# A two-layer hybrid trunk on one core: layer 0's activation rows split by ScalarE and an adding transfer, and its wide products in runs of three

## The chip, the cores and the metric

The kernel runs on one core of a Trainium2 chip. The metric is the device time of one execution in microseconds; the time of a version is the median over its runs. One further execution is recorded by the hardware profiler, and every statement on where time goes is read from that record. The engines are named as the profile names them: PE is TensorE (matrix products; PEld is its loading of weights), DVE is VectorE, ACT is ScalarE, POOL is GpSimd, SP is SyncE, which here only issues transfers.

## The reference

A decoder trunk of two layers over 512 positions of width 1024, in float32. Each layer is a mixer and then a gated feed-forward network with a causal convolution of width 3, both behind an RMS norm and added to the residual. The change lies in the feed-forward network of layer 0:

```python
def gated_conv_ffn(x, w_gate, w_up, conv_w, conv_b, w_down):
    g = jnp.einsum('bsd,df->bsf', x, w_gate)
    g = causal_dwconv3(g, conv_w) + conv_b
    up = jnp.einsum('bsd,df->bsf', x, w_up)
    return jnp.einsum('bsf,fd->bsd', jax.nn.silu(g) * up, w_down)
...
def reference(x, ...):
    h = x
    for layer in range(DEPTH):
        ...
        hn = rms_norm(h, norm_ffn[layer])
        h = h + gated_conv_ffn(hn, w_ffn_gate[layer], w_ffn_up[layer], ...)
    return rms_norm(h, final_norm)
```

D_FF is 2816, that is 22 rows of 128 features. In the kernel a row is a tile of 128 features by 512 positions.

## The kernel before

**Numbers in two parts.** A float32 operand is multiplied as a high part (rounded to the format float32r) plus a low part (the rest, rounded likewise): high x high, high x low and low x high are added up in PSUM. Every operand of a product therefore exists as two tiles, `..._hi` and `..._lo` (weights: `whi_...`, `wlo_...`). There are two ways to make them. In the first, ScalarE copies the source into the high tile and VectorE subtracts: low = source - high (functions `split`, L262, `halves`, L855, and `parts`, L148). In the second, ScalarE copies the source times -1 into the low tile, a transfer on POOL's queue adds the source to it, and ScalarE makes the high tile as well (functions `summed`, L137, and the inner `split` of `prepare`, L884). VectorE has no part in the second.

**The feed-forward stage.** `Ffn.steps` (L1004) runs over the 22 rows two at a time: group f makes the rows f and f+1. Group 0 is computed directly; the groups 2 to 20 are done by a seven-product scheme for two-by-two blocks, once for the gate (`g`) and once for the up-projection (`u`), so 14 products a group. `prepare` builds a group's weight operands (`whi_a`, `whi_s12g`, `wlo_u` and so on) and `products` (L912) runs the 14 products in the order of its list `todo`: g1, u1, g2, g5, g6, u5, u6, g7, u2, u7, g3, u3, g4, u4. The results collect in PSUM banks that are named after gate or up-projection, group and bank, such as `g_10a`; products 1, 6, 7 and 4 of the gate follow each other in the same bank, so each must be taken out (ScalarE's COPY at L944 and VectorE's add at L932) before the next one writes. Each matmul of a product covers a quarter of the contraction.

**Narrow and wide.** A narrow product (L705) issues three matmuls of 256 columns for each quarter. A wide product (L695) issues one of 512 columns for each quarter, in which the high weights meet the high and low parts of the moving operand side by side, and one of 256 columns with the low weights. In layer 0 the products are wide from group 8 on, in part in group 6 (`FIRST_WIDE`, L675); in layer 1 from group 6 on. The order of the two widths is set by the list `parts_of`. Layer 0 alternates: wide, narrow, narrow, wide, and so on, product by product. Layer 1 runs three products' low weights, then three products' high weights.

**After the products.** VectorE and ScalarE turn the gate into a row: multiply by the norm's factor (L968), convolution (`c`, L739 and L741), Silu (`s`, L749), and products with the up-projection (L976 to L983). `STEPS` (L667) says when finished rows become operands: `act` (L752) splits a row `s` into `a_hi` and `a_lo`. Rows 0 and 1 are split after group 0, rows 2 and 3 after group 2, rows 4 and 5 after group 4, then four rows at a time: 6 to 9 after group 8, 10 to 13 after group 12, 14 to 17 after group 16, 18 to 21 at the end. The tiles `a_hi` and `a_lo` have four buffers each. The down-projection of a set of rows (`half_down`, matmuls `d<-a_hi,whi_d` and so on, L156 to L158) comes in two halves, one behind each of the next two groups: rows 6 to 9 are read behind group 10 and again behind group 12.

**What sets the order.** The order of the instructions on each engine is made by a scheduler when the program is built, within the limits of the data and of a few explicit orders (`behind`, L81, which says that one instruction stands after another of the same engine). Each engine then runs its list strictly in order, and waits where an operand or a buffer is not ready. POOL's queue issues the adding transfers in order as well.

Of the kernel before, what the change touches and what calls it, by code (L numbers as in the profile page):

```python
# [9 lines left out]
F32R = mybir.dt.float32r  # L10
BF16 = mybir.dt.bfloat16
AF = mybir.ActivationFunctionType
ALU = mybir.AluOpType
PSUM = bass.MemoryType.PSUM

P = 128
D = 1024
S = 512
# [3 lines left out]
NF = FF // P  # L22
# [9 lines left out]
def tile_trunk(ctx: ExitStack, tc: tile.TileContext, x, norm_mix, norm_ffn, final_norm,  # L32
# [3 lines left out]
    nc = tc.nc  # L36
# [44 lines left out]
    def behind(ins, first):  # L81

        if first is not None:
            tc.add_manual_dep(ins.ins, first.ins.name, mybir.DependencyInfo(
                mybir.DependencyClass.NoSync, mybir.DependencyReason.DATA), reason="order")
# [176 lines left out]
    def split(pool, src, name, scale=1.0, tag="a", bufs=None):  # L262
        hi = pool.tile([P, S], F32R, tag=f"{tag}hi", bufs=bufs, name=f"{name}_hi")
        lo = pool.tile([P, S], F32R, tag=f"{tag}lo", bufs=bufs, name=f"{name}_lo")
        nc.scalar.activation(hi, src, AF.Copy, scale=scale)  # L265
        if isinstance(scale, float):
            nc.vector.tensor_tensor(lo, src, hi.bitcast(F32), ALU.subtract)
        else:
            nc.vector.scalar_tensor_tensor(lo, src, scale, hi.bitcast(F32),
                                           op0=ALU.mult, op1=ALU.subtract)  # L270
        return hi, lo
# [15 lines left out]
    def padded_tile():  # L287
        turn[0] += 1
        return padded[turn[0] % NPADDED]
# [426 lines left out]
    class Ffn:  # L716
# [33 lines left out]
            return s  # L750

        def act(self, ft, s):  # L752
            self.acts[ft] = split(self.ap, s, f"a{self.layer}_{ft}", tag="a", bufs=4)

        def pair_weights(self, order):

# [155 lines left out]
        def products(self, f, stat):  # L912

            layer, ap, n = self.layer, self.ap, f"{self.layer}_{f}"
            banks = {"g": {}, "u": {}}
            kept = ap.tile([P, 3, HALF], F32, tag="kept", bufs=1, name=f"kept{n}")
            pads = [padded_tile() for _ in range(2)]
            lo, hi = slice(2, 2 + HALF), slice(2 + HALF, 2 + S)
            dst = {("g", 1): pads[0][:, lo], ("g", 6): pads[0][:, hi], ("g", 7): pads[1][:, hi],
                   ("g", 4): pads[1][:, lo]}  # L920
            dst.update({("u", product): kept[:, i, :] for i, product in enumerate((1, 6, 7))})
            onto = {2: 1, 7: 7, 3: 6}
            s = {}

            def in_both(key, product):
                first = FIRST_WIDE[layer]
                return f >= first[key] or f == first["g"] and product in (2, 5, 3)

            def add(d, bank, halves):
                ins = None  # L930
                for half in halves:
                    ins = nc.vector.tensor_tensor(d, bank[:, half * HALF : (half + 1) * HALF], d,  # L932
                                                  ALU.add)
                return ins

            def after(key, product, bank):
                halves = range(1 + in_both(key, product))
                if product in onto:
                    ins = add(dst[key, onto[product]], bank, halves)
                    if product == 7:  # L940
                        self.added[key] = ins
                elif (key, product) != ("u", 4):
                    d = dst[key, 7 if product == 5 else product]
                    nc.scalar.copy(d, bank[:, :HALF])  # L944
                    add(d, bank, halves[1:])

            todo = [("g", 1), ("u", 1), ("g", 2), ("g", 5), ("g", 6), ("u", 5), ("u", 6),
                    ("g", 7), ("u", 2), ("u", 7), ("g", 3), ("u", 3), ("g", 4), ("u", 4)]
            if layer and all(in_both(*at) for at in todo):
                parts_of = [(0, (False,))]  # L950
                for i in range(0, len(todo), 3):
                    parts_of += [(j, (True,)) for j in range(i, min(i + 3, len(todo)))]
                    parts_of += [(j, (False,)) for j in range(i + 1, min(i + 4, len(todo)))]
            else:
                parts_of = [(i, (i % 2 == 1, i % 2 == 0)) for i in range(len(todo))]
            begun = set()
            for i, lows in parts_of:
                key, product = todo[i]
                bank = self.multiply(banks[key], f"{key}{n}", product, stat[key, product],
                                     in_both(key, product), lows)  # L960
                if len(lows) == 1 and i not in begun:
                    begun.add(i)
                    continue
                after(key, product, bank)
                if (key, product) in (("g", 4), ("g", 3)):
                    j = product == 4
                    row = pads[j][:, 2:]
                    nc.vector.tensor_tensor(row, row, self.r, ALU.mult)  # L968
                    s[j] = self.silu(self.conv(pads[j], f + j), f + j)
                    if j and layer == 0:  # L970
                        nc.vector.tensor_tensor(s[1], s[1], self.r, ALU.mult)
            if layer == 0:
                nc.vector.tensor_tensor(kept[:, :2, :], kept[:, :2, :],
                                        self.r.rearrange("p (a b) -> p a b", a=2), ALU.mult)
            s0 = s[0].rearrange("p (a b) -> p a b", a=2)
            nc.vector.tensor_tensor(s0, kept[:, :2, :], s0, ALU.mult)  # L976
            nc.vector.tensor_tensor(s[1][:, HALF:], kept[:, 2, :], s[1][:, HALF:], ALU.mult)
            last = bank[:, :HALF]
            if in_both("u", 4):
                last = kept[:, 0, :]  # L980
                nc.scalar.copy(last, bank[:, :HALF])
                add(last, bank, (1,))
            nc.vector.tensor_tensor(s[1][:, :HALF], last, s[1][:, :HALF], ALU.mult)  # L983
            return [(f + 1, s[1]), (f, s[0])]
# [358 lines left out]
    def ffn1(norm):  # L1343
        with tc.tile_pool(name="f1", bufs=1) as ap:
# [108 lines left out]
            def product(p, i, c0=0, c1=512, bank=None):  # L1453
# [14 lines left out]
                return ps  # L1468

            vec, act, pool = nc.vector, nc.scalar, nc.gpsimd  # L1470
            rows_f = [wp.tile([P, D], F32, tag="raw", bufs=4, name=f"yf{t}") for t in range(NT)]
            factor, root = ([ssf[:, t, i : i + 1] for t in range(NT)] for i in (4, 5))
# [91 lines left out]
            refined(0, 1)  # L1564
            taken(7, 1, right)
            scaled(act, 0, left)
            scaled(act, 0, right)
            stored(0, slice(0, D))
            all_but_last(2, right)
# [84 lines left out]
```

## Time and profile before

| | us |
|---|---|
| median of 3 runs (lowest, highest) | 966.77 (966.71, 966.88) |
| the profiled execution | 966.66 |
| its span, first to last instruction | 964.9 |
| first product of the feed-forward stage's groups of layer 0, group 2 | 165.8 |
| last down-projection of that stage begins | 461.1 |

The clock granted to TensorE was 0.999 of full speed over the span. The page calls an engine busy while an instruction of its own runs; a busy TensorE is not TensorE at its peak, so besides its busy share the distances between the starts of its matmuls are read. Idle time of another engine costs nothing unless TensorE waits for it.

### The profile page before, as it was taken

To read this page: it belongs to the slowest core of one execution; us is meant where nothing else is said; L and a number is where in the kernel's file an instruction comes from. 1 tells how busy PE (TensorE), PEld (TensorE's weight loads), DVE (VectorE), ACT (ScalarE), POOL (GpSimd) and SP (SyncE) were. 2 spreads that over 40 slices of the span, in tenths; PEclk is the share of its full clock that TensorE was granted. 3 is DMA by queue.
4 is the path that set the end of the run, shared out by engine and by line. 5 is a ranking of instruction groups with operands and counts; after the bars stand their busy time and mean duration, and the time that the engine had idled before them with its cause. 6 is when DMAs were issued, how large, how long until landed. Compare 5 with 4: busy or idle time off the path is not lost.

```text
span 964.9 us, 14240 instructions
## 1 busy us (share of the span) xinstructions
PE 956.6 (99%) x5155; PEld 826.5 (86%) x5155; DVE 847.2 (88%) x1435; ACT 620.8 (64%) x944; POOL 162.4 (17%) x183
## 2 busy tenths in 40 slices
PE   9999999999999999999999999999999999999997
PEld 7888898998888888888888888989888888888885
DVE  6887988989899998998878689889998989989898
ACT  5524667766576565765487847787765566646676
POOL 2142333111011010110311002321111011110124
PEclk9999999999999999999999999999999999999999
DMA  7442345777777578774452323467776777667865
GB/s 253 146 141 87 66 144 120 179 188 178 176 174 176 153 175 197 164 180 137 131 153 88 109 88 88 138 134 184 186 181 175 182 176 174 167 168 177 207 146 152
DMA packets 95538, 150.47 MB, mean 156 GB/s; under 512 B 5252, under 2 KB 61548, under 8 KB 95468
## 3 DMA queue, kind: packets, MB, share of 16 engines
q1 hardware_dynamic: 77996, 98.69, 32.8%
q0 software_dynamic: 15696, 49.03, 27.8%
q10 hardware_dynamic: 1776, 1.84, 0.6%
q8 instruction: 41, 0.67, 0.3%
q14 instruction: 29, 0.24, 0.1%
HBM read 98.42 MB, written 2.10 MB: 104 GB/s over the span
## 4 chain that ended last, share of the span: by engine, by line
PE 99%; DMA 0%; DVE 0%; issue 0%; SPq 0%; ACT 0%; DVEq 0%
PE dn L156 3%; PE d L157 3%; PE d L156 3%; PE dn L157 3%; PE d L158 3%; PE dn L158 3%; PE vu_a L1166 2%; PE gu L156 2%; PE gu L158 2%; PE gu L157 2%; PE u_2a L705 1%; PE g_2a L705 1%; PE u_4a L705 1%; PE g_6a L695 1%; PE u_12a L695 1%; PE u_16a L695 1%
## 5 line engine op out<-in xcount | busy, mean ns | idle before, releaser
L143 POOL DMA_DIRECT2D wlo_g<-raw_g x20 | 17.2, 860 | 318.8 <-ACT wlo_g L141 66.5
L741 DVE SCALAR_TENSOR_TENSOR c<-rows,prm,c 128x512 f32<-128x512 f32 x88 | 64.9, 746 | 1.2 <-ACT c L739 1.0
L156 PE MATMUL d<-a_hi,whi_d 128*128 128x512 f32 x144 | 56.1, 389 | 0.0
L156 PE MATMUL dn<-whi_dn,a_hi 128*128 128x512 f32 x144 | 56.1, 389 | 0.0
L157 PE MATMUL d<-a_lo,whi_d 128*128 128x512 f32 x144 | 56.1, 389 | 0.0
L157 PE MATMUL dn<-wlo_dn,a_hi 128*128 128x512 f32 x144 | 56.0, 389 | 0.0
L158 PE MATMUL d<-a_hi,wlo_d 128*128 128x512 f32 x144 | 56.0, 389 | 0.0
L158 PE MATMUL dn<-whi_dn,a_lo 128*128 128x512 f32 x144 | 56.0, 389 | 0.0
L856 ACT ACTIVATE whi_a<-raw_g 128x512 fp32r<-128x512 f32 x20 | 12.6, 632 | 67.2 <-PE g_18e L695 9.4
L739 ACT ACTIVATE c<-rows,prm 128x512 f32<-128x512 f32 x44 | 31.3, 714 | 10.2 <-DVE rows L968 10.1
L1371 DVE SCALAR_TENSOR_TENSOR y<-dn,small,y 128x512 f32<-128x512 f32 x40 | 28.0, 749 | 6.7 <-PE dn L158 6.7
L749 ACT ACTIVATE s<-c,prm 128x512 f32<-128x512 f32 x44 | 31.4, 715 | 3.2 <-DVE c L741 3.0
L265 ACT ACTIVATE a_hi<-s 128x512 fp32r<-128x512 f32 x40 | 24.7, 626 | 12.2 <-PE d L158 9.4
L201 ACT ACTIVATE hg<-h,prm 128x512 fp32r<-128x512 f32 x24 | 17.2, 719 | 23.5 <-DVE h L314 17.0
L158 PEld LDWEIGHTS dn<-whi_dn,a_lo 128*128 128x128 f32 x144 | 27.0, 188 | 5.7
L158 PEld LDWEIGHTS d<-a_hi,wlo_d 128*128 128x128 f32 x144 | 27.0, 188 | 5.6
L157 PEld LDWEIGHTS dn<-wlo_dn,a_hi 128*128 128x128 f32 x144 | 27.0, 188 | 5.6
L156 PEld LDWEIGHTS d<-a_hi,whi_d 128*128 128x128 f32 x144 | 27.0, 188 | 5.6
L156 PEld LDWEIGHTS dn<-whi_dn,a_hi 128*128 128x128 f32 x144 | 27.0, 188 | 5.6
L157 PEld LDWEIGHTS d<-a_lo,whi_d 128*128 128x128 f32 x144 | 27.0, 188 | 5.5
L141 ACT ACTIVATE wlo_g<-raw_g 128x1024 fp32r<-128x1024 f32 x20 | 21.0, 1048 | 16.3 <-PE g_2e L705 7.6
L152 DVE TENSOR_TENSOR wlo_d<-raw_d,whi_d 128x1024 fp32r<-128x1024 f32 x18 | 22.0, 1224 | 10.4 <-ACT whi_d L151 10.4
(1279 smaller groups left out, 3377.6 us busy)
## 6 DMA issues: line engine op xcount, KB each, us to landing
raw_g<-in_w_ffn_gate_dram SPq DMA_DIRECT2D x40, 512.0 KB, 3.8
raw_u<-in_w_ffn_up_dram SPq DMA_DIRECT2D x40, 512.0 KB, 3.7
raw_dn<-in_w_ffn_down_dram SPq DMA_DIRECT2D x22, 512.0 KB, 3.5
wlo_g<-raw_g POOLq DMA_DIRECT2D x20, 512.0 KB, 5.2
wlo_u<-raw_u POOLq DMA_DIRECT2D x20, 512.0 KB, 6.1
raw_d<-in_w_ffn_down_dram SPq DMA_DIRECT2D x18, 512.0 KB, 4.1
wlo_s12g<-s12g POOLq DMA_DIRECT2D x18, 512.0 KB, 6.6
wlo_s34g<-s34g POOLq DMA_DIRECT2D x18, 512.0 KB, 6.2
```

Source lines behind the costliest of these rows:

```text
L141: first = nc.scalar.activation(lo, raw, AF.Copy, scale=-1.0)
L152: behind(nc.vector.tensor_tensor(lo, raw, hi.bitcast(F32), ALU.subtract), after[0])
L156: nc.tensor.matmul(ps, lhs[0], rhs[0], start=start, stop=False, skip_group_check=skip)
L157: nc.tensor.matmul(ps, lhs[0], rhs[1], start=False, stop=False, skip_group_check=skip)
L158: nc.tensor.matmul(ps, lhs[1], rhs[0], start=False, stop=stop, skip_group_check=skip)
L265: nc.scalar.activation(hi, src, AF.Copy, scale=scale)
L695: last_matmul[0] = nc.tensor.matmul(ps if low else banks[at], left(kp)[low], right(kp)[0] if low else both(kp), start=first, stop=kp == NP ...
L705: nc.tensor.matmul(ps, l, r, start=first, stop=end, skip_group_check=True)
L739: nc.scalar.activation(c, t[:, 0:S], AF.Copy, scale=prm("cf", ft))
L741: self.last_conv = nc.vector.scalar_tensor_tensor(c, t[:, i : S + i], prm("cf", i * NF + ft), c, op0=ALU.mult, op1=ALU.add)
L749: self.last_silu = nc.scalar.activation(s, c, AF.Silu, bias=self.prm("bf", ft))
L1371: return nc.vector.scalar_tensor_tensor(dst, ps, ffn.cols[:, t : t + 1], dst, op0=ALU.mult, op1=ALU.add)
```

## The change

For the rows 0 to 17 of layer 0, `act` makes the parts in the second way: ScalarE copies the row times -1 into `a_lo`, a transfer on POOL's queue adds the row to it, and ScalarE copies the row into `a_hi`, in that order. The tiles and their four buffers stay the same; rows 18 to 21 and layer 1 keep VectorE's subtraction. And `products` uses the order in runs of three products also in layer 0, in every group whose products are all wide but the last: the groups 8, 10, 12, 14, 16 and 18.

```diff
@@ -750,7 +750,16 @@
         def act(self, ft, s):
-            self.acts[ft] = split(self.ap, s, f"a{self.layer}_{ft}", tag="a", bufs=4)
+            name = f"a{self.layer}_{ft}"
+            if not (self.layer == 0 and ft < NF - 4):
+                self.acts[ft] = split(self.ap, s, name, tag="a", bufs=4)
+                return
+            hi = self.ap.tile([P, S], F32R, tag="ahi", bufs=4, name=f"{name}_hi")
+            lo = self.ap.tile([P, S], F32R, tag="alo", bufs=4, name=f"{name}_lo")
+            first = nc.scalar.activation(lo, s, AF.Copy, scale=-1.0)
+            nc.gpsimd.dma_start(lo, s, accum_op=ALU.add)
+            behind(nc.scalar.activation(hi, s, AF.Copy), first)
+            self.acts[ft] = hi, lo
@@ -946,7 +955,7 @@
             todo = [("g", 1), ("u", 1), ("g", 2), ("g", 5), ("g", 6), ("u", 5), ("u", 6),
                     ("g", 7), ("u", 2), ("u", 7), ("g", 3), ("u", 3), ("g", 4), ("u", 4)]
-            if layer and all(in_both(*at) for at in todo):
+            if (layer or f + 2 < NF) and all(in_both(*at) for at in todo):
                 parts_of = [(0, (False,))]
                 for i in range(0, len(todo), 3):
                     parts_of += [(j, (True,)) for j in range(i, min(i + 3, len(todo)))]
```

Lines behind L762 move down by nine, and the scheduler puts other instructions in another order too. Three places follow; rows of the changed kernel carry its own line numbers.

ScalarE before, from the COPY that empties the last bank of group 8 to the COPY of the first bank of group 10 (`g_10a`) and the two copies behind it. `a_6_hi` to `a_9_hi` are the rows' high parts, the other `whi_...` and `wlo_...` are group 10's weights:

```order
L981 COPY kept_8_2603<-u_8a 128x256
L749 ACTIVATE s_9_2752<-c_9_2748,prm_415 128x512
L265 ACTIVATE a_6_hi<-s_6_2436 128x512
L265 ACTIVATE a_9_hi<-s_9_2752 128x512
L887 ACTIVATE wlo_s34g_10_2884<-s34g_10_2868 128x1024
L889 ACTIVATE whi_s34g_10_2883<-s34g_10_2868 128x1024
L141 ACTIVATE wlo_u_10_1_2894<-raw_u_10_1_2859 128x1024
L265 ACTIVATE a_8_hi<-s_8_2725 128x512
L944 COPY rows_119<-g_10a 128x256
L856 ACTIVATE whi_s12u_10_2891<-s12u_10_2888 128x1024
L145 ACTIVATE whi_u_10_1_2893<-raw_u_10_1_2859 128x1024
```

And with the change, from the same COPY to the COPY of `g_10a`:

```order
L990 COPY kept_8_2609<-u_8a 128x256
L759 ACTIVATE a_6_lo<-s_6_2442 128x512
L761 ACTIVATE a_6_hi<-s_6_2442 128x512
L898 ACTIVATE whi_s34g_10_2893<-s34g_10_2878 128x1024
L141 ACTIVATE wlo_u_10_1_2904<-raw_u_10_1_2869 128x1024
L759 ACTIVATE a_9_lo<-s_9_2758 128x512
L761 ACTIVATE a_9_hi<-s_9_2758 128x512
L865 ACTIVATE whi_s12u_10_2901<-s12u_10_2898 128x1024
L759 ACTIVATE a_8_lo<-s_8_2735 128x512
L761 ACTIVATE a_8_hi<-s_8_2735 128x512
L145 ACTIVATE whi_u_10_1_2903<-raw_u_10_1_2869 128x1024
L953 COPY rows_119<-g_10a 128x256
```

The low parts are copied ahead of the high ones, and `whi_s12u` and `whi_u`, which stood behind the COPY of `g_10a`, now stand ahead of it. Ahead of this piece stand, in the new order, `a_7_lo`, the Silu `s_8`, `a_7_hi`, `wlo_s34g` and the Silu `s_9`; `s_8` stood ahead of `a_7_hi` before. The groups 14 and 18 read alike with their own numbers.

TensorE in group 6, around the second use of the bank `g_6a` (product 6 of the gate, `g_6a<-t`), before:

```order
L695 MATMUL g_6e<-t_0_3_1609,whi_s12g_6_2270 128x512
L695 MATMUL u_6e<-t_0_0_1558,wlo_s12u_6_2291 128x256
L695 MATMUL u_6e<-t_0_1_1576,wlo_s12u_6_2291 128x256
L695 MATMUL u_6e<-t_0_2_1594,wlo_s12u_6_2291 128x256
L695 MATMUL u_6e<-t_0_3_1609,wlo_s12u_6_2291 128x256
L695 MATMUL u_6e<-t_0_0_1558,whi_s12u_6_2290 128x512
L695 MATMUL g_6a<-t_0_1556,whi_s12g_6_2270 128x512
```

And with the change:

```order
L695 MATMUL g_6e<-t_0_2_1594,whi_s12g_6_2276 128x512
L695 MATMUL g_6e<-t_0_3_1609,whi_s12g_6_2276 128x512
L695 MATMUL g_6a<-t_0_1556,whi_s12g_6_2276 128x512
L695 MATMUL g_6a<-t_1_1574,whi_s12g_6_2276 128x512
L695 MATMUL g_6a<-t_2_1592,whi_s12g_6_2276 128x512
```

The five matmuls of `u_6e` that stood ahead of `g_6a` now come behind that product. On ScalarE the copies `a_5_lo`, `a_5_hi`, `a_4_lo` and `a_4_hi` stand directly ahead of the COPY that empties `g_6a`, where `a_5_hi` and `a_4_hi` stood; on VectorE the subtractions `a_5_lo` and `a_4_lo`, which stood ahead of its add into `rows` from `g_6a`, are gone.

POOL's transfers from the second weight operand of group 10 on, before:

```order
L888 DMA wlo_s34g_10_2884<-s34g_10_2868 128x1024
L143 DMA wlo_u_10_1_2894<-raw_u_10_1_2859 128x1024
L143 DMA wlo_g_12_1_3161<-raw_g_12_1_3144 128x1024
L888 DMA wlo_s12g_12_3159<-s12g_12_3154 128x1024
L888 DMA wlo_s34g_12_3171<-s34g_12_3155 128x1024
```

And with the change:

```order
L897 DMA wlo_s34g_10_2894<-s34g_10_2878 128x1024
L760 DMA a_6_lo<-s_6_2442 128x512
L143 DMA wlo_u_10_1_2904<-raw_u_10_1_2869 128x1024
L760 DMA a_9_lo<-s_9_2758 128x512
L760 DMA a_8_lo<-s_8_2735 128x512
L143 DMA wlo_g_12_1_3171<-raw_g_12_1_3154 128x1024
```

The transfer of row 7 stands ahead of this piece, the one of row 6 between two weight operands of group 10, and those of rows 9 and 8 behind them.

## The prediction

> **What bounds the kernel now.** I read the page's busy times and its chain of waits first, to see which engine sets the end.
>
> ```profile
> PE 956.6 (99%) x5155; PEld 826.5 (86%) x5155; DVE 847.2 (88%) x1435; ACT 620.8 (64%) x944; POOL 162.4 (17%) x183
> ...
> PE 99%; DMA 0%; DVE 0%; issue 0%; SPq 0%; ACT 0%; DVEq 0%
> ```
>
> TensorE (PE) works 956.6 of 964.9 us and the chain that ended last is 99% TensorE: the other engines matter only where they make it wait. The change lies in layer 0's feed-forward stage, so next come the busy times of that stretch, and of the same stage of layer 1, which already runs its wide groups in runs of three. The columns are the stretch, its length, then busy time and count of PE, PEld, DVE, ACT and POOL, the clock, the DMA share and GB/s.
>
> ```profile
> 160.00:461.00 301.00, 300.96 (x1709) 264.61 (x1708) 276.40 (x488) 195.17 (x282) 31.82 (x37) 1.00 0.70 172
> 640.00:940.00 300.00, 300.00 (x1653) 261.98 (x1652) 272.26 (x485) 197.15 (x291) 36.97 (x43) 1.00 0.73 176
> ```
>
> TensorE is idle for 0.04 of 301 us there, at full granted clock. So this stage gains only by cheaper matmuls or by removing the rare slow spots inside the pipeline. Of waits that end on other engines, two are recorded: one at the start of the program, one in the wide-matmul line (L695).
>
> ```profile
> PE z L417 <- ACT whi_z L410: 0.3, 1, 0.3
> ...
>   DVE rows L932: 0.4, 1
> ```
>
> **Part 1, runs of three products.** No product is added or removed; matmuls of equal width stand together longer, so TensorE changes width less often. Layer 0's group 12 (first six rows, the last being what follows it) and layer 1's group 10 (last three) show both orders with the same 14 wide products; columns are start, duration, operation.
>
> ```profile
> 308.89 1.07 PE L695 MATMUL g_12a<-hg,whi_a 128*128 128x512 f32 x4
> 309.80 0.64 PE L695 MATMUL g_12a<-hg,wlo_a 128*128 128x256 f32 x4
> 310.27 0.64 PE L695 MATMUL u_12a<-hg,wlo_a 128*128 128x256 f32 x4
> 310.75 1.09 PE L695 MATMUL u_12a<-hg,whi_a 128*128 128x512 f32 x4
> 311.68 1.07 PE L695 MATMUL g_12b<-hg,whi_g 128*128 128x512 f32 x4
> ...
> 328.44 0.39 PE L156 MATMUL d<-a_hi,whi_d 128*128 128x512 f32 x1
> ...
> 756.20 1.07 PE L695 MATMUL g_10a<-hg,whi_a 128*128 128x512 f32 x4
> ...
> 760.38 1.07 PE L695 MATMUL g_10e<-t,whi_s12g 128*128 128x512 f32 x4
> ...
> 775.71 0.39 PE L156 MATMUL dn<-whi_dn,a_hi 128*128 128x512 f32 x1
> ```
>
> Layer 0: 328.44 - 308.89 = 19.55 us. Layer 1: 775.71 - 756.20 = 19.51 us. The row at 310.75 shows why: a wide run behind a narrow one takes 0.93 us to the next start (311.68), one at the head 0.91 (308.89 to 309.80), so each change of width costs 0.02 us and layer 1 has two fewer (five for seven). Groups 8, 10, 12, 14, 16 and 18 change: 6 x 0.04 = **-0.24 us** (bounds by the rows' rounding, -0.18 to -0.30).
>
> [...]
>
> **Part 2, the rows' low parts.** Eighteen rows (0 to 17) lose a VectorE subtraction and gain a ScalarE copy and an adding transfer from POOL's queue. Prices:
>
> ```profile
> L267 DVE TENSOR_TENSOR a_lo<-s,a_hi x40: 679/684/693, 177.5 to 879.2; 128x512 fp32r<-128x512 f32 x40
> ...
> L265 ACT ACTIVATE a_hi<-s 128x512 fp32r<-128x512 f32 x40 | 24.7, 626 | 12.2 <-PE d L158 9.4
> ...
> L143 POOL DMA_DIRECT2D wlo_g<-raw_g x20 | 17.2, 860 | 318.8 <-ACT wlo_g L141 66.5
> ...
> t<-t POOLq DMA_DIRECT2D x4, 256.0 KB, 3.7
> ...
> wlo_s12g<-s12g POOLq DMA_DIRECT2D x18, 512.0 KB, 6.6
> ...
> q0 software_dynamic: 15696, 49.03, 27.8%
> ```
>
> VectorE loses 18 x 0.684 = 12.3 us of its 276.4; ScalarE gains 18 x 0.626 = 11.3 (195 to 206 of 301); POOL gains 18 x 0.86 = 15.5 (32 to 47). The transfers move 18 x 0.262 = 4.7 MB; at q0's rate that is 4.7/49.03 x 27.8% x 964.9 = 26 us of all 16 engines, which takes the DMA share from 0.70 to about 0.79. A row of 256 KB has no row of its own on this path: between the 3.7 us of the 256 KB transfers and the 6.6 us of the 512 KB ones I take 5. None of this is on TensorE, so its price is 0 where cover holds. Three places decide.
>
> *Group 6.* Here stands the 0.4 us wait. Bank g_6a must be emptied by VectorE before TensorE's product 6 writes it.
>
> ```profile
> 222.69 0.63 PE L695 MATMUL u_6e<-t,wlo_s12u 128*128 128x256 f32 x4
> 223.16 0.40 PE L695 MATMUL u_6e<-t,whi_s12u 128*128 128x512 f32 x1
> 223.60 1.19 PE L695 MATMUL g_6a<-t,whi_s12g 128*128 128x512 f32 x4
> ...
> 219.69 1.14 ACT L265 ACTIVATE a_hi<-s 128x512 fp32r<-128x512 f32 x2
> 220.73 0.35 ACT L944 COPY rows<-g_6a 128x256 f32<-128x256 f32 x1
> ...
> 220.72 1.29 DVE L267 TENSOR_TENSOR a_lo<-s,a_hi 128x512 fp32r<-128x512 f32 x2
> ...
> 223.13 0.42 DVE L932 TENSOR_TENSOR rows<-g_6a,rows 128x256 f32<-128x256 f32 x1
> ```
>
> The add ended at 223.55 and TensorE started at 223.60, 0.21 us after its pitch of 0.23 from 223.16, with a first run 1.19 - 1.07 = 0.12 longer: 0.33 us in all. The change takes the two subtractions (1.29 us) from in front of the add, but puts two more copies in front of ScalarE's COPY: from 219.69 four at 0.52 (1.04 to the next start for two) end at 221.77, the COPY at 222.12, the add by 222.6. The new order also asks for the bank earlier, at 222.69. I take the wait as gone with 0.1 us to spare: **-0.33 us**. If the copies take 0.626 each, 0.43 us more, the wait is back in full: bounds -0.33 to 0.
>
> *The groups in which four rows are split, 10, 14 and 18.* ScalarE's order there has eight row copies before the first bank's COPY.
>
> ```profile
> 270.04 1.05 ACT L145 ACTIVATE whi_g<-raw_g 128x1024 fp32r<-128x1024 f32 x1
> 270.99 0.61 ACT L265 ACTIVATE a_hi<-s 128x512 fp32r<-128x512 f32 x1
> ...
> 275.92 0.63 ACT L265 ACTIVATE a_hi<-s 128x512 fp32r<-128x512 f32 x1 [2.09 <-PE d L158]
> ...
> 280.02 0.37 ACT L944 COPY rows<-g_10a 128x256 f32<-128x256 f32 x1
> ...
> L749 ACT ACTIVATE s<-c,prm 128x512 f32<-128x512 f32 x44 | 31.4, 715 | 3.2 <-DVE c L741 3.0
> ...
> 279.25 0.68 DVE L267 TENSOR_TENSOR a_lo<-s,a_hi 128x512 fp32r<-128x512 f32 x1
> ...
> 281.05 0.42 DVE L932 TENSOR_TENSOR rows<-g_10a,rows 128x256 f32<-128x256 f32 x1
> 281.66 1.23 DVE L857 TENSOR_TENSOR wlo_s12u<-s12u,whi_s12u 128x1024 fp32r<-128x1024 f32 x1 [0.19 <-ACT whi_s12u L856]
> ...
> 278.44 1.07 PE L695 MATMUL g_10a<-hg,whi_a 128*128 128x512 f32 x4
> ...
> 284.02 1.07 PE L695 MATMUL g_10a<-t,whi_s12g 128*128 128x512 f32 x4
> ```
>
> The first copy (270.99) found its tile free; s_8's Silu now stands behind it, so the low part's copy starts about 0.6 us earlier, at 270.4. Up to the COPY the new queue holds eight row copies (8 x 0.52), two Silu (2 x 0.72), one small COPY (0.35) and five copies of 128x1024 (5 x 0.95, from 270.04 to 270.99): 10.7 us, so it starts at 281.1 instead of 280.02, the 2.09 us of idle before 275.92 having been filled. On VectorE wlo_s12u and two 0.68 us operations now precede the add: 279.25 + 1.23 + 2 x 0.68 = 281.84, the add ends at 282.3. TensorE wants the bank at 284.02 - 0.04: 1.7 us to spare, against 2.5 before (281.47). **0 us.** Behind the waiting copies stand the Silus, then VectorE's gate products; they come some 2.5 us later, and feed rows that are split a group later. POOL's transfer of a row stands ahead of wlo_u's: by the same sum wlo_u's copy ends at 276.8, issue 0.86 and landing 6.6 give 284.3, and its product, the ninth, comes about 10 us into the group, at 288.
>
> *The rows themselves.* The last low part is copied before 281.1 and lands by 281.1 + 0.86 + 6.6 = 288.6; the down-projection that reads these rows follows group 10, at 298.0 (group 10 starts 278.44 and takes 19.5). Ten us hide it. Were that cover gone, the price is what is late beyond 298. The rows' source tiles stay taken until the landing too, and are rewritten only by the Silus after group 10.
>
> **Sum.** The profiled execution took 966.66 us, of which 964.9 is span; the 1.8 us around it stay. 966.66 - 0.24 - 0.33 = 966.1. The median of the runs is 0.11 above that execution: **966.2 us**, 0.06% below 966.77. About 0.2% (1.9 us) is what a measurement of this kernel can tell from no change, so I call it the same.
>
> **Rivals.**
> *The small gains do not come, or small waits return* (22%). Group 6 has 0.1 us to spare; and with runs of three the product that reuses g's first bank comes about 2.3 us (0.91 + 3 x 0.47) after that bank is complete instead of 2.8, an interval that ScalarE's COPY and VectorE's add must fit. Against it: layer 1 has the same runs and no idle TensorE (300.00 of 300.00) with VectorE as full. At 0.2 us in six groups, without the 0.33: 966.5 + 1.2 = 967.7, still the same. Runs that are worth nothing in layer 0 (966.44) belong here too.
> *ScalarE becomes the bound at the split groups, slower* (7%). It decides from the point where the COPY is 1.7 us later than I have it, for instance if the copies again wait for the down-projection's last matmuls as at 275.92. With the margin used up and the four extra copies uncovered, 3 groups x 4 x 0.626 = 7.5: 973.7. Against it: it is idle 106 of 301 us there.
> *The transfers starve, slower* (2%). POOL's issue would have to be held while VectorE works, until the rows miss 298.0. At 1 us late in each of the four down-projections behind split rows, 966.2 + 4 = 970. Against it: VectorE is busy 92% of this stretch, and the median issue is 0.86 us and landing 6.6 at most.
> [...]
> *VectorE was the pace after all, faster* (3%). If its 12.3 us came off the end: 954. Its 92% speaks for it; the 0.04 us of TensorE idle against.
> *As forecast*: 66%, with 965.9 to 966.5 of its own.
>
> The range, 965.8 to 967.6, takes in both terms' bounds and most of the small waits. Faster by over 0.2% is the last rival, 0.03; slower the two slower ones and the tail of the small waits, 0.10; the same 0.87.
>
> **What would show it.** Right: each of the six groups takes 19.51 us from first matmul to the down-projection; no wait of TensorE in L695 for g_6a; VectorE's busy time about 835 and ScalarE's about 632; rows' transfers landing over 5 us before their down-projection. Wrong: a TensorE wait on ScalarE's COPY or VectorE's L932 (line numbers shift) in groups 10, 14, 18, or on a_lo; or a stage shorter by more than 0.6 us.

## The result, and the profile after

| | us |
|---|---|
| before, median of 19 runs (lowest, highest) | 966.58 (966.09, 967.62) |
| with the change, median of 19 runs (lowest, highest) | 967.81 (966.65, 970.54) |
| ratio, with its 95% interval | 1.0017 (1.0011 to 1.0023) |
| the profiled execution with the change | 969.49, span 967.6 |

The change costs 1.2 us by the medians (0.13%; by the means it is 0.17%, which is the ratio in the table). That is still within the 0.2% that the prediction calls the same, but the interval leaves out a ratio of 1, the time is just outside the range (967.6 was its upper end), and the sign is against the forecast of 0.06% faster. The longest run lies 2.7 us over the median, before it was 1.0. The profiled execution is one of the long ones, 2.83 us over the 966.66 us of the execution profiled before. So its trace shows the loss larger than the median does, and it has to be asked what of it is common to all runs.

The page of the changed kernel, busy times and the chain that ended last:

```profile
PE 957.6 (99%) x5155; PEld 827.8 (86%) x5155; DVE 839.5 (87%) x1417; ACT 628.0 (65%) x962; POOL 178.2 (18%) x201
...
PE 90%; DVE 4%; DMA 2%; ACT 2%; issue 1%; POOL 0%; DVEq 0%; SPq 0%; ACTq 0%
```

The work moved as described: VectorE down, ScalarE and POOL up. But the chain, which was 99% TensorE, now leaves TensorE for 10% of the span. The waits of TensorE say where:

```profile
PE g_6a L695 <- DVE rows L941: 2.0, 1, 2.0
```

One wait, at group 6, and it is the one that the forecast took as gone. TensorE's rows round it (start, duration, operation, idle time and its releaser):

```profile
216.54 1.07 PE L695 MATMUL g_6a<-hg,whi_a 128*128 128x512 f32 x4
...
221.24 1.09 PE L695 MATMUL g_6e<-t,whi_s12g 128*128 128x512 f32 x4
224.35 1.19 PE L695 MATMUL g_6a<-t,whi_s12g 128*128 128x512 f32 x4 [2.02 <-DVE rows L941]
225.38 0.65 PE L695 MATMUL g_6a<-t,wlo_s12g 128*128 128x256 f32 x4
225.85 1.02 PE L695 MATMUL u_6e<-t,wlo_s12u 128*128 128x256 f32 x4
226.68 1.91 PE L695 MATMUL u_6e<-t,whi_s12u 128*128 128x512 f32 x4
...
240.08 0.40 PE L156 MATMUL d<-a_hi,whi_d 128*128 128x512 f32 x1
```

The group takes 240.08 - 216.54 = 23.54 us; before it took 20.03. Of the 3.5 us more, 2.02 are the wait. The rest is in the rows behind it: the four wide matmuls at 226.68 take 1.91 us where the four at 221.24 took 1.09. The windows of that stretch (length, TensorE's busy time and count, granted clock, DMA share, GB/s) show why:

```profile
222.00:226.00 4.00, 1.98 (x11) 0.98 1.02 167
226.00:230.00 4.00, 4.00 (x20) 0.59 1.05 256
```

The granted clock fell to 0.59 on the mean of those 4 us, where it was 1.00 before.

The chain in order of time shows what VectorE was late for. These are its pieces from group 4 into group 6:

```profile
192.58 7.49 DMA wlo_u<-raw_u
200.21 6.25 DMA raw_g<-in_w_ffn_gate_dram
206.48 0.69 DVE s12g L886
207.51 0.60 DVE s12g L888
...
209.65 0.60 DVE s12u L886
```

It goes back through VectorE's sums of group 6 to a transfer: `raw_g`, the load of group 6's gate weights, and from its issue to the landing of group 4's `wlo_u`. VectorE could read `raw_g` at 206.48, where before the same row stood at 204.77:

```profile
204.77 0.69 DVE L877 TENSOR_TENSOR s12g<-raw_g,raw_g 128x512 f32<-128x512 f32 x1 [0.64 <-DMA raw_g<-in_w_ffn_gate_dram]
```

That is 1.71 us later. The COPY of `g_6a`, for which VectorE's add waits, is later by more, 223.49 against 220.73 = 2.76 us: 1.71 from the load, and the other 1.05 is about what the two copies take that now stand ahead of it (2 x 0.52).

The load ahead of `raw_g` on SP's queue, `raw_u`, is late too. Its issue and ScalarE's first use of it, before:

```profile
196.69 0.37 SPq L129 DMA_DIRECT2D raw_u<-in_w_ffn_up_dram  x1
...
202.44 0.64 ACT L856 ACTIVATE whi_a<-raw_u 128x512 fp32r<-128x512 f32 x1
```

and with the change, with VectorE's row behind it:

```profile
195.81 0.37 SPq L129 DMA_DIRECT2D raw_u<-in_w_ffn_up_dram  x1
...
204.25 0.63 ACT L865 ACTIVATE whi_a<-raw_u 128x512 fp32r<-128x512 f32 x1 [2.23 <-DMA raw_u<-in_w_ffn_up_dram]
...
204.91 0.69 DVE L866 TENSOR_TENSOR wlo_a<-raw_u,whi_a 128x512 fp32r<-128x512 f32 x1 [2.43 <-ACT whi_a L865]
```

It was issued 0.88 us earlier than before and first used 1.81 us later, with a wait where there had been none. VectorE lost most of its time there: behind it, it waited only 0.55 us for `raw_g`. So `raw_u` was slow (8.44 us from its issue to its first use, before 5.75), and not issued late. `raw_g` was issued 1.68 us later (200.21 against 198.53) and took as long until it was read as before (6.27 us against 6.24), so for this load the two profiles alone do not tell a late issue from a slow transfer; the experiments have to.

What could be in the way of the loads is in the same stretch of POOL's queue. The two adding transfers of rows 3 and 2:

```profile
195.26 0.86 POOL L760 DMA_DIRECT2D a_lo<-s  x1 [1.83 <-ACT a_lo L759]
196.57 0.86 POOL L760 DMA_DIRECT2D a_lo<-s  x1 [0.45 <-ACT a_lo L759]
```

From 198 to 204 us three loads of 512 KB for group 6 are under way on SP's queue (q1). Packets, MB and share of the 16 transfer engines in these 6 us, before:

```profile
q1 hardware_dynamic: 1332, 1.33, 77.9%
...
q0 software_dynamic: 2, 0.00, 0.0%
```

and with the change:

```profile
q0 software_dynamic: 275, 0.51, 53.0%
q1 hardware_dynamic: 990, 0.99, 50.5%
```

The loads moved 0.99 MB where they had moved 1.33, and POOL's queue moved 0.51 MB where it had moved nothing: the end of `wlo_u`, which landed at 200.07, and the rows. The 0.34 MB that the loads lost are 1.5 us at the rate of before. That is an estimate; the later issue of `raw_g` is in it too.

### The profile page after: what moved, and what is told of

Its sections match the earlier page's. It is cut to its first block, busy times and chain, and to the rows that moved or that the text cites. A ratio compares the mean times of both kernels' runs of the same rounds, so it can differ in the third digit from the quotient of the medians.

```text
span 967.6 us, 14302 instructions
## 1 busy us (share of the span) xinstructions
PE 957.6 (99%) x5155; PEld 827.8 (86%) x5155; DVE 839.5 (87%) x1417; ACT 628.0 (65%) x962; POOL 178.2 (18%) x201
## 4 chain that ended last, share of the span: by engine, by line
PE 90%; DVE 4%; DMA 2%; ACT 2%; issue 1%; POOL 0%; DVEq 0%; SPq 0%; ACTq 0%
PE dn L156 3%; PE dn L158 3%; PE dn L157 3%; PE d L156 3%; PE d L158 3%; PE d L157 3%; PE vu_a L1175 2%; PE u_20a L695 1%; PE u_18a L695 1%; PE g_18a L695 1%; PE u_12a L695 1%; PE g_12a L695 1%; PE u_10a L695 1%; PE g_10a L695 1%; PE u_16a L695 1%; PE g_16a L695 1%
## 5 line engine op out<-in xcount | busy, mean ns | idle before, releaser
L212 POOL TENSOR_TENSOR ssq_m<-ssq_m,sq_m 128x512 f32<-128x512 f32 x14 | 19.7, 1404 | 64.8 <-ACT sq_m L211 64.8
L314 DVE TENSOR_TENSOR h<-d,h 128x512 f32<-128x512 f32 x40 | 26.9, 689 | 4.2 <-PE d L158 4.1
L145 ACT ACTIVATE whi_u<-raw_u 128x1024 fp32r<-128x1024 f32 x20 | 21.0, 1052 | 14.4 <-PE dn L158 9.6
```

The source lines that it names most:

```text
L145: behind(nc.scalar.activation(hi, raw, AF.Copy), first)
L212: nc.gpsimd.tensor_tensor(self.ssq, self.ssq, sq, ALU.add)
L314: nc.vector.tensor_tensor(h[k], ps, h[k], ALU.add)
```

## The experiments

Three causes were set against each other at first. **L** (late landing): the transfers of rows 2 and 3 delay group 4's `wlo_u`; its landing frees the buffer into which `raw_g` of group 6 is loaded, and group 6 starts late. **S**: ScalarE's two further copies of rows 4 and 5 ahead of the COPY of `g_6a`, with TensorE's earlier demand for the bank. **R**: the runs of three. Two more came from the first results. **B** (bytes): the rows' transfers share the transfer engines with group 6's loads, whatever `wlo_u` does. **C**: ScalarE's copies of rows 2 and 3 and the order round them. All edits are to the changed kernel. The loss to be explained is 1.2 us; against a version that does what was forecast it is some 1.4.

**Runs of three alone** (e1_runs_alone).

```diff
-            if not (self.layer == 0 and ft < NF - 4):
+            if True:
```

> Runs of three alone; all low parts by VectorE as before. Every theory: the six groups 8 to 18 take 19.51 us each instead of 19.55, group 6 keeps its 20.0 us with the 0.3 us wait, and the median is 966.3 us (966.58 of before less 0.25). If it is 967 or more, the loss comes from the runs of three and both theories on group 6 fall.

Measured: 967.86 us (966.68 to 968.89) against 966.66, ratio 1.0010 (1.0002 to 1.0019). Every theory missed this. Group 6, whose instructions stand in the order of before, had its `raw_g` read at 204.20 and took 19.77 us, less than the 20.0 that were expected. Four of the six later groups took 19.51 us, but group 14 took 19.74 and group 18 20.13. In group 18, two rows of VectorE and one of TensorE:

```profile
401.85 1.28 DVE L267 TENSOR_TENSOR a_lo<-s,a_hi 128x512 fp32r<-128x512 f32 x2
...
409.89 0.42 DVE L941 TENSOR_TENSOR rows<-g_18a,rows 128x256 f32<-128x256 f32 x1
...
410.37 0.74 PE L695 MATMUL g_18a<-t,wlo_s34g 128*128 128x256 f32 x4 [0.27 <-DVE rows L941]
```

The third product in bank `g_18a` waits for VectorE's add, which ends at 410.31; VectorE still has the subtractions of rows, two of them at the group's start. In group 14 the same product comes just behind the add too. That the subtractions are the cause is tested by rows 6 to 17 alone, below. The two groups lose 0.85 us together, while the median lies 1.36 us over that kernel's; this profile does not show the rest.

**Rows 2 and 3 by VectorE** (e3_rows23_vector).

```diff
-            if not (self.layer == 0 and ft < NF - 4):
+            if not (self.layer == 0 and ft < NF - 4) or ft in (2, 3):
```

> The change, but rows 2 and 3 (split in group 4) by VectorE, so that their two adding transfers are gone. Theory L (late landing: these two transfers delay group 4's wlo_u, whose landing lets raw_g of group 6 be loaded): wlo_u of group 4 lands about 5.4 us after its issue instead of 7.5, the wait of TensorE for g_6a shrinks from 2.0 us to 0.4 or less, group 6 takes at most 20.2 us instead of 23.5, and the median is 966.3 us (966.0 to 966.7). Theory S (ScalarE: the two more copies of rows 4 and 5 ahead of the COPY of g_6a, with TensorE's earlier demand for the bank): the wait stays at 1 us or more and the median at 967.5 or more.

Measured: 966.42 us (965.66 to 966.96) against 966.66, ratio 0.9997 (0.9988 to 1.0006). TensorE no longer waits in group 6, which takes 237.00 - 217.30 = 19.70 us; all six later groups take 19.51. VectorE reads `raw_g` early:

```profile
204.28 0.68 DVE L886 TENSOR_TENSOR s12g<-raw_g,raw_g 128x512 f32<-128x512 f32 x1
```

S falls: the copies of rows 4 and 5 and TensorE's new order are all still there.

**Rows 4 and 5 by VectorE** (e4_rows45_vector). The same line with `ft in (4, 5)`.

> The change, but rows 4 and 5 (split in group 6) by VectorE: the two copies ahead of the COPY of g_6a are gone, TensorE's order in group 6 is that of before, and the transfers of rows 2 and 3 stay. Theory L: wlo_u of group 4 still lands 7 us or more after its issue, everything of group 6 is some 1.7 us late, TensorE waits 1 us or more there, and the median is 967.3 to 969. Theory S: group 6 takes 20.0 us as before and the median is 966.3 us.

Measured: 967.97 us (967.24 to 970.80), ratio 1.0017 (1.0008 to 1.0026). VectorE read `raw_g` at 206.68, held up by `raw_u` this time: ScalarE waited 2.43 us for it. That load was issued at 196.43, before `wlo_u` had landed, so L has no account of its delay. The wait stayed although ScalarE has no more to do there than before:

```profile
PE g_6a L695 <- DVE rows L941: 1.8, 1, 1.8
```

**Rows 6 to 17 alone** (e5_from_row6).

```diff
-            if not (self.layer == 0 and ft < NF - 4):
+            if not (self.layer == 0 and 6 <= ft < NF - 4):
```

> The change for rows 6 to 17 alone, rows 0 to 5 by VectorE, runs of three kept. Both theories: nothing of groups 2 to 6 differs from before, so group 6 takes 20.0 us; groups 8 to 18 take 19.51 us with no wait in the groups 10, 14 and 18; median 966.3 us. If it is 967 or more, the later rows cost something too that the profile of the changed kernel does not show.

Measured: 966.50 us (965.92 to 967.20), ratio 1.0000 (0.9991 to 1.0009); group 6 took 19.77 us and not the 20.0 expected, the six others 19.51. It differs from the runs alone only in these rows' low parts, and the waits of groups 14 and 18 are gone: in these two groups the runs of three were worth their 0.04 us only with VectorE rid of the subtractions. In group 18 VectorE's add comes at 408.01 instead of 409.89:

```profile
408.01 0.42 DVE L941 TENSOR_TENSOR rows<-g_18a,rows 128x256 f32<-128x256 f32 x1 [1.12 <-ACT rows L953]
...
409.70 0.64 PE L695 MATMUL g_18a<-t,wlo_s34g 128*128 128x256 f32 x4
```

**Low parts alone** (e2_parts_alone).

```diff
-            if (layer or f + 2 < NF) and all(in_both(*at) for at in todo):
+            if layer and all(in_both(*at) for at in todo):
```

> The low parts of rows 0 to 17 as in the change, layer 0's wide groups in the old alternating order. Theory L (the adding transfers of rows 2 and 3 make group 6 late): group 6 waits for g_6a by 1 us or more as in the changed kernel, the groups 8 to 18 take 19.55 us, and the median is 968.0 us (967.81 of the change plus the 0.25 that the runs save). Theory R (the 1.2 us of the change come from the runs of three, since these alone cost as much): 966.6 us or less.

Measured: 968.42 us (967.95 to 969.58), ratio 1.0020 (1.0011 to 1.0029), a wait of 1.6 us for `g_6a`, `raw_g` read at 206.17. The six later groups took 19.55 us. R falls: without the runs the loss is no smaller.

**Rows 2 and 3 alone** (e6_only_rows23).

```diff
-            if not (self.layer == 0 and ft < NF - 4):
+            if not (self.layer == 0 and ft in (2, 3)):
```

> The kernel before with one thing added: rows 2 and 3 by ScalarE and adding transfers. No runs of three in layer 0. Theory L: these two transfers are enough; wlo_u of group 4 lands 7 us or more after its issue instead of 5.4, TensorE waits 1 us or more for g_6a, and the median is 967.3 to 968.5 us. Theory R: 966.6 us, wait of 0.4 us or less.

The text on record describes the kernel wrongly: the runs of three were left in, so it is to be read beside the runs alone (967.86), not beside the kernel before. Measured: 969.27 us (968.65 to 971.26), ratio 1.0028 (1.0016 to 1.0039). It has the waits of groups 14 and 18, and a new one of 1.1 us for `g_6a`: group 6 takes 21.10 us, 1.33 more than with the runs alone, about the 1.41 by which the medians differ. `raw_g` was read at 206.22. But `wlo_u` of group 4 landed 5.5 us after its issue, against 5.4 before, and `raw_g` was issued at 199.00, early, and read 7.2 us later. So the loss comes without the link on which L rests.

**Two transfers that nobody reads** (x1_spare_transfers). Rows 2 and 3 by VectorE, and in `act` (left out here: where rows 0 and 1 are split, ScalarE fills the spare tiles):

```diff
+                if self.layer == 0 and ft in (2, 3):
+                    n = S if ft == 2 else HALF
+                    behind(nc.gpsimd.dma_start(self.spare[ft], s[:, :n], accum_op=ALU.add),
+                           last_added[0])
```

> As e3_rows23_vector (the change with rows 2 and 3 by VectorE, 966.4 us), with two adding transfers whose result nobody reads (256 and 128 KB, three quarters of the bytes of rows 2 and 3) on POOL's queue behind group 4's wlo_u, where the rows' transfers stood. Theory L by bytes alone: wlo_u of group 4 lands 6.8 us or more after its issue, TensorE waits again for g_6a by 0.7 to 2 us, median 967.1 to 968.3 us. Theory C (the four ScalarE copies of rows 2 and 3 and the order round them cost the time, the transfers nothing): no wait, 966.4 us.

Measured: 967.46 us (966.54 to 968.81), ratio 1.0010 (1.0001 to 1.0018). It tells nothing of group 6: there was no wait for `g_6a`, `raw_g` was read at 205.11, 0.83 us later than without the transfers, of which 0.48 is that all of group 6 began later (217.78 against 217.30). The transfers went out at 193.88, since they had no copy of ScalarE to wait for. And TensorE waited 0.6 us in group 2 (`u_2a` on a copy of ScalarE), which had the spare tiles to fill as well: the edit brought a wait of its own.

**The rows' transfers later** (x2_late_transfers). `self.taken` holds the copies of `products`, so group 4's of `u_4a` here.

```diff
             first = nc.scalar.activation(lo, s, AF.Copy, scale=-1.0)
+            if ft in (2, 3):
+                behind(first, self.taken["u", 6])
```

> The change, with ScalarE's copies of rows 2 and 3 held back behind its copy of u_4a, so that their transfers are issued near 204 us instead of 195 and 197. As many copies, transfers and bytes as the change. Theory L: wlo_u of group 4 lands about 5.5 us after its issue and raw_g of group 6 is issued near 199 us; TensorE's wait for g_6a is 0.4 us or less and the median 966.0 to 966.6 us. If the number of transfers or copies is what costs, wherever they stand, it stays at 967.5 us or more.

Measured: 966.50 us (965.61 to 967.88), ratio 0.9999 (0.9990 to 1.0008), no more than the small wait of before in group 6 (0.4 us by line L695). As many copies, transfers and bytes as the change; the transfers are issued at 203.66 and 204.69. `raw_g` was issued at 200.48, as late as in the change, because `wlo_u` landed 6.9 us after its issue; yet VectorE read it at 204.58. From 200 to 204 us POOL's queue moved nothing here, and 0.29 MB in the change. The number of transfers is not what costs, and L's link is refuted from the other side too. ScalarE's copies moved along with the transfers, so this run does not tell B from C; the next one does.

**The bytes by themselves** (x3_spare_bytes). Rows 2 and 3 by VectorE; transfers behind ScalarE's high copies, tiles zeroed by POOL (left out here):

```diff
+                if self.layer == 0 and ft in (2, 3):
+                    n = S if ft == 3 else HALF
+                    nc.gpsimd.dma_start(self.spare[ft], self.acts[ft][0].bitcast(F32)[:, :n],
+                                        accum_op=ALU.add)
```

> As e3_rows23_vector (no wait for g_6a, raw_g of group 6 read by VectorE from 204.3 us on), with two adding transfers of 256 and 128 KB into tiles that nobody reads, issued behind ScalarE's copies of rows 3 and 2, so at about the moment at which the change issues those rows' transfers; the tiles are zeroed by POOL ahead of group 2's row transfers, so no engine but POOL has more to do. Theory B (the bytes share the transfer engines with group 6's loads): three quarters of the change's delay of 2.2 us, so raw_g is read from 205.7 to 206.1 us on; the wait for g_6a is back, 0.3 to 1.2 us; median 966.7 to 967.6 us. Theory C (ScalarE's copies and the order round them): 204.3 us, no wait, 966.4 us.

Measured: 967.34 us (966.44 to 968.81) against 966.72, ratio 1.0006 (0.9997 to 1.0015). By its interval the time cannot be told from no change; the trace can. The row that tells:

```profile
205.94 0.69 DVE L894 TENSOR_TENSOR s12g<-raw_g,raw_g 128x512 f32<-128x512 f32 x1 [0.63 <-DMA raw_g<-in_w_ffn_gate_dram]
```

and the wait:

```profile
PE g_6a L695 <- DVE rows L949: 0.7, 1, 0.7
```

All inside what B expected; C expected 204.3 and no wait. In the 6 us from 198 the two queues moved

```profile
q0 software_dynamic: 315, 0.44, 54.5%
q1 hardware_dynamic: 977, 0.98, 49.8%
```

which is the picture of the change again, without its copies on ScalarE. C, which expects no wait, falls.

**The change once more** (c1_change_again).

> The change once more, for a second profile of it. Theory B: raw_g of group 6 is read by VectorE after 206 us again, and TensorE waits 1 to 2.2 us for g_6a. If TensorE's clock is halved behind a wait of 2.0 us and not behind 1.8 (as in the profiles so far), the group takes 21.5 to 22 us where the wait is under 1.9 us, and 23.3 us or more where it is over 2.0.

Measured: 967.76 us (967.33 to 968.28), ratio 1.0010 (1.0000 to 1.0020); `raw_g` read at 206.37, wait 1.3 us, group 6 21.33 us, 0.2 under the expected 21.5, with the clock whole:

```profile
222.00:226.00 4.00, 2.66 (x15) 1.00 1.01 165
226.00:230.00 4.00, 4.00 (x29) 1.00 1.05 268
```

This execution took 967.86 us, near the median of the change, so it is nearer the usual case than the first profile: 21.33 - 19.70 (rows 2 and 3 by VectorE) = 1.63 us, and the medians differ by about 1.4.

In all, sorted by the moment at which VectorE reads `raw_g` of group 6:

| kernel | `raw_g` issued, us | read, us | wait for `g_6a`, us | group 6, us | median, us |
|---|---|---|---|---|---|
| runs alone | 199.21 | 204.20 | none listed | 19.77 | 967.86 (waits in 14, 18) |
| rows 2, 3 by VectorE | 199.19 | 204.28 | none listed | 19.70 | 966.42 |
| rows 6 to 17 alone | 199.71 | 204.29 | none listed | 19.77 | 966.50 |
| transfers later | 200.48 | 204.58 | none listed | 19.91 | 966.50 |
| before | 198.53 | 204.77 | none listed | 20.03 | 966.58 |
| spare transfers | 199.15 | 205.11 | none listed | 19.70 | 967.46 (wait in 2) |
| bytes by themselves | 199.59 | 205.94 | 0.7 | 20.64 | 967.34 |
| low parts alone | 199.75 | 206.17 | 1.6 | 21.56 | 968.42 |
| rows 2, 3 alone | 199.00 | 206.22 | 1.1 | 21.10 | 969.27 (waits in 14, 18) |
| the change, again | 200.21 | 206.37 | 1.3 | 21.33 | 967.76 |
| the change | 200.21 | 206.48 | 2.0 | 23.54 | 967.81 |
| rows 4, 5 by VectorE | 200.82 | 206.68 | 1.8 | 21.82 | 967.97 |

(The waits are those that the list of TensorE's waits names; a listing of line L695 alone also has 0.4 us before and with the later transfers, and 0.2 in runs alone and rows 6 to 17 alone.) Read at 205.1 or earlier, there is no wait in the list; from 205.9 on there is one. The moment of the issue does not sort them: read late were loads issued at 199.00 and at 200.82, read early one issued at 200.48. The bytes account for about 1.25 us of group 6 by the transfers into spare tiles (20.64 - 19.70 = 0.94 for three quarters of them, scaled up in proportion, which is an estimate) and 1.33 by rows 2 and 3 alone, out of 1.63 in the change's second profile. What makes up the other 0.3 us stays open. So does this: in the five profiles in which rows 0 to 3 all go the new way, `wlo_u` of group 4 landed 6.9 to 7.5 us after its issue, in the others 5.4 to 6.4; and group 4's `wlo_g`, which lands before the transfers of rows 2 and 3 are issued, was late there too (6.8 to 7.4 us against 5.9 to 6.2).

Three versions, rows 2 and 3 by VectorE, rows 6 to 17 alone, and the late transfers, are 1.3 to 1.4 us below the change and cannot be told from the kernel before. None is faster than the kernel before by more than the measurement resolves.

## Why the prediction was wrong

*The runs of three*: the term was right. In the change all six groups took the 19.51 us that was forecast, as group 12 shows:

```profile
311.78 1.07 PE L695 MATMUL g_12a<-hg,whi_a 128*128 128x512 f32 x4
...
331.29 0.39 PE L156 MATMUL d<-a_hi,whi_d 128*128 128x512 f32 x1
```

What the prediction did not say is that the term hangs on Part 2 in two of the groups. It priced the shorter distance to the bank's next use at nothing because layer 1 has it without a wait; alone in layer 0 it costs 0.23 us in group 14 and 0.62 in group 18. The first rival names that interval.

*Groups 10, 14 and 18*: right, no wait. Group 10 began 281.38 - 278.44 = 2.94 us later than before, and with that taken off, the COPY that was forecast for 281.1 came at 284.05 - 2.94 = 281.11 and the bank was free at 285.08 - 2.94 = 282.14 (forecast 282.3), 1.9 us ahead of TensorE. That the COPY fits to the hundredth is luck: the first row copy came at 273.65 - 2.94 = 270.71 instead of 270.4, and the queue from there to the COPY took 10.40 us instead of 10.7. The rows:

```profile
284.05 0.35 ACT L953 COPY rows<-g_10a 128x256 f32<-128x256 f32 x1
...
284.66 0.42 DVE L941 TENSOR_TENSOR rows<-g_10a,rows 128x256 f32<-128x256 f32 x1
...
286.94 0.64 PE L695 MATMUL g_10a<-t,wlo_s12g 128*128 128x256 f32 x4
```

*Prices*: 18 copies of 0.62 us and 18 issues, as forecast, but a mean issue of 0.92 us instead of 0.86 and landings well over the 5 us that were taken:

```profile
L760 POOL DMA_DIRECT2D a_lo<-s x18 | 16.5, 919 | 25.6 <-ACT a_lo L759 21.8 <-ACT s L749 3.5 <-issue 0.4
...
L759 ACT ACTIVATE a_lo<-s 128x512 fp32r<-128x512 f32 x18 | 11.2, 623 | 0.0
...
a_lo<-s POOLq DMA_DIRECT2D x18, 256.0 KB, 7.4
```

That these transfers of 256 KB took longer on the median (7.4 us) than those of 512 KB for `wlo_u` and `wlo_s12g` (6.6) fits what 198 to 204 us showed for the rows 2 and 3: they did not run alone (53.0% and 50.5%). VectorE's busy time fell by 7.7 us (847.2 to 839.5) where 12.3 were forecast, and ScalarE's rose by 7.2 (620.8 to 628.0) where 11.3 were. Neither sets the time here. The rows themselves had the cover that was claimed for them, and no down-projection waited.

*Group 6*: wrong, and here the prediction failed. The walk along ScalarE and VectorE holds when it is taken by itself: with rows 2 and 3 by VectorE, the four copies and the COPY leave the bank free in time and group 6 takes 19.70 us, 0.33 less than before. But most of that is not the gain that the term of -0.33 claims. Runs alone and rows 6 to 17 alone, which leave group 6 in the order of before, take 19.77; there VectorE reads `raw_g` at 204.20 and 204.29, and only in the execution before at 204.77, after a wait of 0.64 us for it. So 0.26 of the 0.33 came and went with that load, in one execution, and 0.07 us is left for the change.

The step that failed is the one above it, in the prices of Part 2: what "takes the DMA share from 0.70 to about 0.79" is not on TensorE, "so its price is 0 where cover holds. Three places decide." The runs showed a price of 1.3 to 1.4 us by the medians for two of the eighteen transfers, those of rows 2 and 3. The share was a mean over 301 us. In the stretch that mattered the transfer engines had no room, as windows of the trace of before show:

```profile
184.00:190.00 6.00, 0.94 (x2) 1.00 1.00 234
190.00:196.00 6.00, 1.72 (x2) 1.00 1.04 234
196.00:202.00 6.00, 0.00 (x0) 1.00 0.90 217
```

(the last two columns are DMA share and GB/s, those ahead POOL's busy time and the clock). Two rows now go out at the end of 12 us at full share, and three loads queue up beside them; for one of these, `raw_g`, VectorE had already waited before. The walk looked at the places where the moved instructions stand on ScalarE, VectorE and POOL, and never at group 4, where they stand on the transfer engines.

*The rivals*: the one on transfers had 2% and the wrong mechanism. It asked whether POOL's issue would be held and the rows come late for their down-projection; the issues took 0.86 us on the median and the rows were in time. What came late was another user of the same engines. Its price of 4 us would have been too high for the median as well. The first rival, small waits, gave 967.7 us, close to the 967.81 measured; but it had waits in six groups for the bank's shorter interval, where the change has one wait at group 6 for another reason. That agreement is luck.

*The clock* was in no term: in the first profile of the change, with a wait of 2.02 us, TensorE's granted clock was 0.59 over 226 to 230 us and its matmuls there took 1.5 us longer; in the second, with a wait of 1.3 us, the clock was 1.00 there.

## What to carry to other kernels

A transfer that replaces an instruction is not free because its own result has time; here two of eighteen cost 1.3 to 1.4 us. Ask which loads are under way when it goes out, in windows of a few us, and what the last of them releases. The mean share of 0.70 before was made of stretches at 1.00 (184 to 190 us) and stretches at 0.16 (182 to 184 us), and moving the same two transfers, with their copies, by 8 us removed their whole cost (966.50 us against 966.52 before). Two edits can also carry each other: in groups 14 and 18 the shorter bank distance alone cost 0.23 and 0.62 us, and it paid (19.51 us) once the other edit had taken the rows' subtractions off VectorE, so each is to be tried alone and together.

## What the runs showed of the hardware

*TensorE's granted clock fell to 0.50 behind a wait of 2.02 us, in one execution.* It was 0.50 from 226 to 229 us, and the matmuls between 225.85 and 229.50 took 1.54 us longer than the same ones in the change's second profile. Behind waits of 1.1, 1.3, 1.6 and 1.8 us, each in one execution, it was 1.00, as in the kernel with rows 4 and 5 by VectorE (wait 1.8):

```profile
226.00:230.00 4.00, 4.00 (x28) 1.00 0.82 244
```

Whether the length of the wait alone decides is not shown. The spans of the change's 19 runs fall into two sets, fourteen from 964.9 to 966.8 us and five from 967.6 to 968.8, of which the profiled one (967.6) belongs to the second. Whether the other four also lost the clock was not profiled; their mean clock (0.996 or 0.997) does not tell, since the second profile has 0.997 as well, with the clock whole in group 6.

*Two queues shared the transfer engines, in no fixed proportion.* From 198 to 204 us, in the change, the packets of POOL's queue took 53.0% of the time of the 16 engines and those of SP's 50.5%, where SP's alone had taken 77.9% before; with the bytes by themselves it was 54.5% and 49.8%, in the change's second profile 68.3% and 38.1%. These are sums over 6 us; the order in which an engine took the packets of the two queues is not shown.
